# Forgetting attention on one core: the gates' rows on ScalarE's DMA queue, the weight piece asked for at unit 0

## The chip, the core and the metric

The kernel runs on one core of a Trainium2 chip. The metric is the device time of one execution in microseconds (us). The core has five instruction streams: TensorE (PE; PEld is its weight load), VectorE (DVE), ScalarE (ACT), GpSimd (POOL) and SyncE (SP). Each executes its own instructions in their order and waits for the others on semaphores. DMAs are issued by SP, POOL or ACT, as instructions of that stream. A DMA that has to wait holds up everything behind it in the same stream.

## What is computed

A two-layer decoder trunk over 512 positions of width 1024. Layer 0 has dilated window attention, layer 1 has forgetting attention, and each is followed by a gated convolutional feed-forward part. The change lies in forgetting attention: 16 heads of width 64, causal, with a bias made of the cumulative log of the forget gates, c.

```python
def fox_mixer(xn, w_q, w_o, k, v, c):
    q = (xn @ w_q).reshape(B, T, B_HEADS, HEAD_DIM)
    ...
    for i in range(T // BLK):                       # BLK = 128 queries
        s = jnp.einsum('bqhd,bkhd->bhqk', q[:, q0:q1], k[:, :q1]) * scale
        s = s + (c_t[:, :, q0:q1, None] - c_t[:, :, None, :q1])
        s = jnp.where(causal, s, NEG)
        p = jax.nn.softmax(s, axis=-1)
        outs.append(jnp.einsum('bhqk,bkhd->bqhd', p, v[:, :q1]))
    return jnp.concatenate(outs, axis=1).reshape(B, T, B_WIDTH) @ w_o
```

## The kernel before

All products are made from split operands: each float32 matrix is a high part and a low part, and a product is three matmuls (`mm3`, lines 267 to 269).

**The stage.** Forgetting attention runs over 32 units, (j,i) for head pair j = 0..7 and query block i = 0..3; unit (j,i) sees 128(i+1) keys. The loop over n (line 1585 on) is a software pipeline written out by hand, and each engine executes its instructions in the order in which the loop body issues them. For unit n the body issues: the scores on PE (`f_scores`, line 1509); the division of unit n-1 by its row sums on DVE (`f_norm`, 1528 and 1530); the biased scores and their maximum on DVE (1518) and the exponentials on ACT (1520), both in `f_exp`; the bias of unit n+1 on POOL (`f_bias`, 1492 and 1493); a quarter of the query projection of a later pair on PE (`q_part`); the transposes of unit n-2 on PE with their copies on ACT (`f_transpose`, 1542 and 1544). Every fourth unit the products with the values of the preceding pair are made (`f_pv`, 1557).

**The gates' rows (ck).** The cumulative gates lie in DRAM as 16 rows of 512 (`cd`). `load_ck(j)` (line 1399) reads the two rows of pair j into all 128 partitions, 512 KB, in one DMA on SP's queue (1402). Pair j+1's rows are asked for at unit (j,0). Their readers are the four biases of pair j+1; the first of these is issued at unit (j,3).

**The query copies (qst).** At unit (j,0) ACT makes the high part of the queries of pair j+1 (1426), at (j,1) DVE the low part (1434). Then two DMAs swap the halves between partitions 0-63 and 64-127 (1437, 1438). They are on SP's queue for pairs 1 to 6, on POOL's for 0 and 7. The scores of unit (j+1,0) need them.

**The weight pieces (wraw).** `Weights` brings every weight in pieces of 512 KB. `load(n)` issues DMAs on SP's queue (46) until n pieces are under way; `high` (54) first calls `load` for its own piece and `ahead_dma` (here 1) more, then rounds a piece to its high part on ACT. The low part is a subtraction on DVE (`low`, 66), or, in pairs 2 to 5, a negated copy on ACT (`minus`, 61) and an accumulating DMA from POOL's queue which reads the raw piece (`low_added`, 81). `high` runs at unit (j,1) of pairs 0 and 1, at the end of unit (j,0) of pairs 2 to 5, and at (6,1), (6,2) and (6,3) of the last pieces; `low_added` at unit (j,1).

**Buffers.** The tiles wraw, ck, bias and prob (the probabilities of a unit) share one pool, t4, of ten buffers. A new tile takes a buffer whose last reader is done; whichever instruction writes it first waits for that reader. A raw piece is freed by its low part, ck by the last bias of its pair (issued at (j,2)), a bias by its unit's step on DVE, prob by its transposes two units later.

Of the kernel before, what the change touches and what calls it, by code (L numbers as in the profile page):

```python
# [15 lines left out]
T = 512  # L16
# [84 lines left out]
def trunk_kernel(ctx, tc, x, norm_gains, w_qkv_a, w_o_a, w_q_b, w_o_b, kv_norm, w_kvf, b_f,  # L101
                 w_up, conv_w, conv_b, w_down, rope, out):
    nc = tc.nc
    act, dve, pool, pe, sp = nc.scalar, nc.vector, nc.gpsimd, nc.tensor, nc.sync
# [8 lines left out]
    def t8(shape, dt=F32, name="t8"):  # L113
        return p8.tile(shape, dt, tag="t8", name=name)

    def t4(shape, dt=F32, name="t4"):
        return p4.tile(shape, dt, tag="t4", name=name)
# [82 lines left out]
    W = Weights(nc, new_raw, lambda: t8([128, 2, 1024], F32R, name="w"), pieces)  # L200
# [1157 lines left out]
    def values(banks, w, s, blocks):  # L1358
        for b in blocks:
            for k in range(2):  # L1360
                kc = 2 * s + k
                ah, al = xs(bd2.xT, kc, slice(b * 128, b * 128 + 128))
                mm3(banks[b], ah, al, w[0][:, k, :], w[1][:, k, :], kc == 0, kc == KD - 1)

    def value_weight():
        return [t.rearrange("p (k c) -> p k c", k=2) for t in W.get()]
# [29 lines left out]

    cks = {}

    def load_ck(j):
        t = t4([128, 2, T], name="ck")  # L1400
        s = cd[2 * j:2 * j + 2, :]
        sp.dma_start(t, bass.AP(tensor=s.tensor, offset=s.offset, ap=[[0, 128], [T, 2], [1, T]]))
        cks[j] = t

    qT = {}
# [2 lines left out]
    def q_part(j, i):  # L1408

        if j >= 8:  # L1410
            return
        if i == 0:
            qps[j] = (bank([128, T], name="q_ps"), [t.rearrange("p (k c) -> p k c", k=8) for t in W.get()])
        o, (wh, wl) = qps[j]
        for kc in (2 * i, 2 * i + 1):
            bh, bl = xs(xTq, kc, ALL)
            mm3(o, wh[:, kc, :], wl[:, kc, :], bh, bl, kc == 0, kc == KD - 1)

    def q_high(j):
        if j >= 8:  # L1420
            return
        o = qps[j][0]
        qT[j] = t = t8([128, 2, 2, T], F32R, name="qst")
        for hh in range(2):
            own, _ = halves(hh)
            act.copy(t[own, 0, hh], o[own])

    def q_low(j):
        if j >= 8:
            return  # L1430
        o, t = qps.pop(j)[0], qT[j]
        for hh in range(2):
            own, other = halves(hh)
            dve.tensor_tensor(t[other, 0, hh], o[own], t[own, 0, hh].bitcast(F32), ALU.subtract)

        queue = sp if 0 < j < 7 else pool
        queue.dma_start(t[0:64, 1].bitcast(F32), t[64:128, 0].bitcast(F32))
        queue.dma_start(t[64:128, 1].bitcast(F32), t[0:64, 0].bitcast(F32))
# [26 lines left out]
    for s in range(4):  # L1465
        values(banks, value_weight(), s, range(4))
        next(down1, None)
        if s == 0:
            W.ahead = 2
            q_part(0, 0)  # L1470
            q_part(0, 1)
            load_ck(0)
        elif s == 1:
            q_part(0, 2)
        elif s == 2:
            q_part(0, 3)
            q_high(0)
            q_low(0)
# [8 lines left out]
    def f_bias(j, i):  # L1487
        n = (i + 1) * 128
        bias = t4([128, 2, T], name="bias")
        for hh in range(2):  # L1490
            hd = 2 * j + hh
            pool.tensor_scalar(bias[:, hh, :n], cks[j][:, hh, :n], -1.0, cq[:, i, hd:hd + 1], ALU.mult, ALU.add)
        pool.affine_select(bias[:, :, n - 128:n], bias[:, :, n - 128:n], pattern=[[0, 2], [-1, 128]],
                           compare_op=ALU.is_ge, fill=NEG, base=0, channel_multiplier=1)
        bia[j, i] = bias

    def f_scores(j, i):
        n = (i + 1) * 128
        nn = max(n, 256)
        if i < 2:  # L1500
            o = bank([128, 2, 256], name="s_ps")
            s = [o[:, hh] for hh in range(2)]
        else:
            s = [bank([128, T], name="s_ps") for _ in range(2)]
        for hh in range(2):
            hd = 2 * j + hh
            k = kst[hd // 4][:, hd % 4, :nn]
            for m in range(2):
                pe.matmul(s[hh][:, :nn], qT[j][:, m, hh, i * 128:(i + 1) * 128], k, start=m == 0, stop=m == 1)  # L1509
        return s  # L1510

    def f_exp(j, i, s):
        n = (i + 1) * 128
        bias = bia.pop((j, i))
        p = t4([128, 2, T], name="prob")
        nm, ls = small(2, "nm"), small(2, "ls")
        for hh in range(2):
            dve.tensor_tensor_reduce(p[:, hh, :n], s[hh][:, :n], bias[:, hh, :n], -0.125, BIG, ALU.add, ALU.min,
                                     nm[:, hh:hh + 1])
            act.activation(p[:, hh, :n], p[:, hh, :n], AF.Exp, bias=nm[:, hh:hh + 1], scale=-1.0,  # L1520
                           accum_out=ls[:, hh:hh + 1])
        prob[j, i] = (p, ls)

    def f_norm(j, i):
        n = (i + 1) * 128
        p, ls = prob[j, i]
        rl = small(2, "rl")
        dve.reciprocal(rl, ls)
        for hh in range(2):
            dve.tensor_scalar(p[:, hh, :n], p[:, hh, :n], rl[:, hh:hh + 1], None, ALU.mult)  # L1530
# [3 lines left out]
    def f_transpose(j, i):  # L1534
        p, _ = prob.pop((j, i))
        for hh in range(2):
            if i >= 2 or hh == 0:
                o = bank([128, 4, 128], name="pT_ps")
                t = t2([128, 4, 128], name="pT")
            k0 = (i + 1) * hh if i < 2 else 0  # L1540
            for k in range(i + 1):
                pe.transpose(o[:, k0 + k, :], p[:, hh, k * 128:(k + 1) * 128], ident)  # L1542
            if i >= 2 or hh == 1:
                act.copy(t[:, :k0 + i + 1], o[:, :k0 + i + 1])
            pT[j, i, hh] = t[:, k0:k0 + i + 1]
# [4 lines left out]
    def f_pv(j, i):  # L1550
        if i == 0:
            ops[j] = bank([128, T], name="o_ps")
        o = ops[j]
        for k in range(i + 1):
            for hh in range(2):
                hd = 2 * j + hh
                pe.matmul(o[64 * hh:64 * hh + 64, i * 128:(i + 1) * 128],  # L1557
                          Vt[hd // 8][:, k, (hd % 8) * 64:(hd % 8) * 64 + 64], pT[j, i, hh][:, k, :],
                          start=k == 0, stop=k == i)
        del pT[j, i, 0], pT[j, i, 1]  # L1560

    def f_out_high(j):
        o = ops[j]
        if j % 2 == 0:
            OTb[j // 2] = t8([128, 2, 2, T], F32R, name=f"OTb{j // 2}")
        t = OTb[j // 2]
        act.copy(t[:, 0, j % 2, :], o)

    def f_out_low(j):
        o, t = ops.pop(j), OTb[j // 2]  # L1570
        dve.tensor_tensor(t[:, 1, j % 2, :], o, t[:, 0, j % 2, :].bitcast(F32), ALU.subtract)
# [13 lines left out]
    for n in range(N + 3):  # L1585
        live = n < N
        if live:
            j, i = units[n]
            if i == 0 and j + 1 < 8:
                load_ck(j + 1)  # L1590
            s = f_scores(j, i)
        if 1 <= n <= N:
            f_norm(*units[n - 1])
        if live:
            f_exp(j, i, s)
            if n + 1 < N:
                f_bias(*units[n + 1])
            if i == 1:
                q_low(j + 1)
                if 2 <= j < 6:  # L1600
                    W.minus()
                    W.low_added()
            if i == 2 and j < 2 or (j, i) >= (6, 2):
                W.low()
            if i == 3 and j:
                f_out_low(j - 1)
            q_part(j + 1 + (i > 0), (i + 3) % 4)
        if 2 <= n < N + 2:
            f_transpose(*units[n - 2])
        if n >= N + 3 - len(fill):  # L1610
            po.both(*fill[n - N - 3 + len(fill)])

        if n % 4 == 2 or n == N:
            while pv_next < n - 2:
                ju, iu = units[pv_next]
                pv_next += 1
                f_pv(ju, iu)
                if iu == 3:
                    f_out_high(ju)
        if live and i == 0:  # L1620
            q_high(j + 1)
        if live and (i == (j < 2) if j < 6 else (j, i) >= (6, 1) and W.n_split < wo + 4):
            W.high()
# [51 lines left out]
```

## Time and profile before

| | |
|---|---|
| time, three runs | 1121.34, 1122.23, 1122.56 us; median 1122.23 |
| the profiled execution's own time | 1121.25 us |
| its span in the profile | 1119.2 us |
| granted TensorE clock, mean | 0.998 |
| the edited stage | about 627 to 735 us of the span |
| ScalarE busy over the whole span | 615.7 us, 55% |

Times in the profile are counted from the start of the span. A row of a timeline gives start, duration, engine, line, operation, tile written and tiles read, the number of instructions merged into the row, and in brackets the idle time of the engine just before it with what ended that time. "SPq" is the instruction stream of SP: the duration of such a row is that of the issue, not of the transfer. A row of waits gives who waited for whom, the sum in us, how often, and the longest. Busy times of PE are modelled ends of pipelined matmuls.

### The profile page before, as it was taken

To read this page: it belongs to the slowest core of one execution; us is meant where nothing else is said; L and a number is where in the kernel's file an instruction comes from. 1 tells how busy PE (TensorE), PEld (TensorE's weight loads), DVE (VectorE), ACT (ScalarE), POOL (GpSimd) and SP (SyncE) were. 2 spreads that over 40 slices of the span, in tenths; PEclk is the share of its full clock that TensorE was granted. 3 is DMA by queue.
4 is the path that set the end of the run, shared out by engine and by line. 5 is a ranking of instruction groups with operands and counts; after the bars stand their busy time and mean duration, and the time that the engine had idled before them with its cause. 6 is when DMAs were issued, how large, how long until landed. Compare 5 with 4: busy or idle time off the path is not lost. (4 is left out here: it accounts for less than half of the span.)

```text
span 1119.2 us, 17259 instructions
## 1 busy us (share of the span) xinstructions
PE 1108.2 (99%) x6259; PEld 950.2 (85%) x6259; DVE 891.1 (80%) x1453; ACT 615.7 (55%) x1036; POOL 182.7 (16%) x277
## 2 busy tenths in 40 slices
PE   9999999999999999999999999999999999999997
PEld 6988889889899888888878888789889889888886
DVE  6577788888888689997697777848888888589994
ACT  5444575545445457576462688745445445456572
POOL 1832101200000121000001545500300000121000
PEclk9999999999999999999999999999999999999999
DMA  9469864343433699893447666374333443599862
GB/s 323 149 212 407 323 176 134 94 119 104 139 121 116 158 359 368 299 323 110 132 151 273 198 165 169 105 207 130 96 102 115 132 125 121 151 352 368 319 245 75
DMA packets 179183, 217.34 MB, mean 194 GB/s; under 512 B 11225, under 2 KB 131017, under 8 KB 179098
## 3 DMA queue, kind: packets, MB, share of 16 engines
q1 hardware_dynamic: 169594, 183.99, 50.2%
q0 software_dynamic: 9504, 32.25, 9.1%
q8 instruction: 49, 0.80, 0.3%
q14 instruction: 36, 0.29, 0.1%
HBM read 166.08 MB, written 39.63 MB: 184 GB/s over the span
## 5 line engine op out<-in xcount | busy, mean ns | idle before, releaser
L597 ACT ACTIVATE bb<-up,conv 128x512 f32<-128x512 f32 x80 | 60.6, 775 | 148.6 <-DVE up L927 76.2
L66 DVE TENSOR_TENSOR w<-wraw,w 128x1024 fp32r<-128x1024 f32 x98 | 125.1, 1306 | 18.3 <-ACT w L54 17.8
L267 PE MATMUL acc<-w 128*128 128x512 f32 (+1 forms) x311 | 120.7, 388 | 0.3 <-DVE mix L314 0.3
L269 PE MATMUL acc<-w 128*128 128x512 f32 (+1 forms) x311 | 120.5, 388 | 0.1
L54 ACT CAST w<-wraw 128x1024 fp32r<-128x1024 f32 x110 | 111.5, 1047 | 15.8 <-PE v_ps L268 6.9
L267 PE MATMUL up<-xbh,w 128*128 128x512 f32 (+1 forms) x292 | 104.9, 359 | 0.0
L268 PE MATMUL up<-xcl,w 128*128 128x512 f32 (+1 forms) x292 | 104.9, 359 | 0.0
L267 PE MATMUL up<-xch,w 128*128 128x512 f32 (+1 forms) x292 | 104.9, 359 | 0.0
L268 PE MATMUL up<-xbl,w 128*128 128x512 f32 (+1 forms) x292 | 104.9, 359 | 0.0
L269 PE MATMUL up<-xbh,w 128*128 128x512 f32 (+1 forms) x292 | 104.7, 359 | 0.0
L269 PE MATMUL up<-xch,w 128*128 128x512 f32 (+1 forms) x292 | 104.7, 359 | 0.0
L268 PE MATMUL acc<-w 128*128 128x512 f32 (+1 forms) x267 | 103.3, 387 | 0.0
L613 POOL DMA_DIRECT2D hD<-hc x42 | 24.2, 577 | 317.7 <-DVE hc L615 316.6
L267 PEld LDWEIGHTS acc<-w 128*128 128x128 f32 x311 | 58.4, 188 | 12.6 <-DVE mix L314 0.7
L269 PEld LDWEIGHTS acc<-w 128*128 128x128 f32 x311 | 58.4, 188 | 12.4 <-DVE w L725 0.6
L598 DVE SCALAR_TENSOR_TENSOR bb<-up,conv,bb 128x511 f32<-128x511 f32 x80 | 59.5, 744 | 7.7 <-ACT bb L597 7.7
L268 PE MATMUL up<-xsl,w 128*128 128x256 f32 x224 | 63.4, 283 | 0.0
L267 PE MATMUL up<-xsh,w 128*128 128x256 f32 x224 | 63.4, 283 | 0.0
L269 PE MATMUL up<-xsh,w 128*128 128x256 f32 x224 | 63.4, 283 | 0.0
L267 PEld LDWEIGHTS up<-xbh,w 128*128 128x128 f32 x292 | 55.1, 189 | 8.3
L600 DVE SCALAR_TENSOR_TENSOR bb<-up,conv,bb 128x510 f32<-128x510 f32 x80 | 59.9, 749 | 2.8
L267 PEld LDWEIGHTS up<-xch,w 128*128 128x128 f32 x292 | 55.1, 189 | 8.3
(303 smaller groups left out, 3017.5 us busy)
## 6 DMA issues: line engine op xcount, KB each, us to landing
wraw<-in_w_up_dram SPq DMA_DIRECT2D x88, 512.0 KB
dT<-dsums SPq DMA_DIRECT2D x24, 512.0 KB
dsums<-in_w_down_dram SPq DMA_DIRECT2D x22, 512.0 KB
dsums<-in_w_down_dram SPq DMA_DIRECT2D x44, 256.0 KB
hD<-hc POOLq DMA_DIRECT2D x44, 256.0 KB, 4.7
dact<-hD SPq DMA_DIRECT2D x44, 256.0 KB
wraw<-dT SPq DMA_DIRECT2D x22, 512.0 KB
wraw<-in_w_down_dram SPq DMA_DIRECT2D x22, 512.0 KB
```

Of the source, the lines that this page charges most:

```text
L54: self.nc.scalar.copy(pair[:, 0], raw)
L66: self.nc.vector.tensor_tensor(pair[:, 1], raw, pair[:, 0].bitcast(F32), ALU.subtract)
L267: pe.matmul(o, ah, bh, start=first, stop=False, skip_group_check=shared)
L268: pe.matmul(o, ah, bl, start=False, stop=False, skip_group_check=shared)
L269: pe.matmul(o, al, bh, start=False, stop=last, skip_group_check=shared)
L597: act.activation(bb[:, s, :], ps, AF.Identity, bias=cp[:, 3, ch:ch + 1], scale=cp[:, 2, ch:ch + 1])
L598: dve.scalar_tensor_tensor(bb[:, s, 1:], ps[:, :T - 1], cp[:, 1, ch:ch + 1], bb[:, s, 1:], ALU.mult, ALU.add)
L600: dve.scalar_tensor_tensor(bb[:, s, 2:], ps[:, :T - 2], cp[:, 0, ch:ch + 1], bb[:, s, 2:], ALU.mult, ALU.add)
L613: pool.dma_start(hD[c - 1], hc.pop(c - 1))
```

## The change

`load_ck` takes the queue as an argument. The load of pair 0, ahead of the loop, stays on SP's queue; the seven loads in the loop are issued by ACT. At the same place, unit 0 of pairs 0 to 6, `W.load` is called for as many pieces as the next `high` would ask for, so that `high` finds its DMA already issued.

```diff
-    def load_ck(j):
+    def load_ck(j, queue):
         t = t4([128, 2, T], name="ck")
         s = cd[2 * j:2 * j + 2, :]
-        sp.dma_start(t, bass.AP(tensor=s.tensor, offset=s.offset, ap=[[0, 128], [T, 2], [1, T]]))
+        queue.dma_start(t, bass.AP(tensor=s.tensor, offset=s.offset, ap=[[0, 128], [T, 2], [1, T]]))
         cks[j] = t
...
             q_part(0, 1)
-            load_ck(0)
+            load_ck(0, sp)
...
             j, i = units[n]
             if i == 0 and j + 1 < 8:
-                load_ck(j + 1)
+                load_ck(j + 1, act)
+                W.load(W.n_split + 1 + W.ahead_dma)
             s = f_scores(j, i)
```

## The prediction

> **What bounds the kernel now.** I read the page first, then the waits of TensorE over the whole span, then the chain of waits and the timelines of the forgetting-attention stage (627 to 735 us), because only that stage is edited.
>
> ```profile
> span 1119.2 us, 17259 instructions
> PE 1108.2 (99%) x6259; PEld 950.2 (85%) x6259; DVE 891.1 (80%) x1453; ACT 615.7 (55%) x1036; POOL 182.7 (16%) x277
> ```
>
> TensorE (PE) is busy for all but 11 us of the span. No edit that removes waits can gain more than that, and only waits inside this stage are in reach. These are the ones of the stage:
>
> ```profile
> PE s_ps L1509 <- DMA qst<-qst: 1.3, 3, 0.7
> PE pT_ps L1542 <- ACT w L54: 0.6, 1, 0.6
> ```
>
> Three times the scores wait for the copies of the query pair between partitions (qst), once a transpose waits. The timeline of PE places them; I call unit i of head pair j "(j,i)".
>
> ```profile
> 635.87 0.36 PE L1509 MATMUL s_ps<-kst,qst 128*128 128x256 f32 x1
> 636.45 0.59 PE L1509 MATMUL s_ps<-kst,qst 128*128 128x256 f32 x3 [0.21 <-DMA qst<-qst]
> ...
> 649.17 0.36 PE L1509 MATMUL s_ps<-kst,qst 128*128 128x256 f32 x1
> 649.86 0.59 PE L1509 MATMUL s_ps<-kst,qst 128*128 128x256 f32 x3 [0.33 <-DMA qst<-qst]
> ...
> 662.58 0.71 PE L1509 MATMUL s_ps<-kst,qst 128*128 128x256 f32 x4
> ...
> 675.42 0.72 PE L1509 MATMUL s_ps<-kst,qst 128*128 128x256 f32 x4
> ...
> 711.71 0.28 PE L1509 MATMUL s_ps<-kst,qst 128*128 128x256 f32 x1
> 712.70 0.60 PE L1509 MATMUL s_ps<-kst,qst 128*128 128x256 f32 x3 [0.71 <-DMA qst<-qst]
> ...
> 716.47 1.30 PE L1542 MATMUL pT_ps<-ident,prob 128*128 128x128 f32 x8 [0.62 <-ACT w L54]
> ```
>
> Matmuls overlap, so the bracket understates a stall. Undisturbed, four scores take 0.71 us and the last alone 0.28, so they follow each other at (0.71 - 0.28)/3 = 0.14 us. The real stalls are 636.45 - 635.87 - 0.14 = 0.44 us at (1,0), 649.86 - 649.17 - 0.14 = 0.55 at (2,0), and 0.85 at (7,0). Without stalls PE needs 675.42 - 662.58 = 12.84 us for a head pair. ScalarE (ACT) and VectorE (DVE) pass each unit's softmax to and fro at the same pace: the first exponential of pairs 3 and 4 is 677.19 - 664.38 = 12.81 us apart.
>
> ```profile
> 662.91 0.59 ACT L1544 COPY pT<-pT_ps 128x512 f32<-128x512 f32 x1
> 664.38 0.40 ACT L1520 ACTIVATE prob<-prob,nm 128x128 f32<-128x128 f32 x1 [0.89 <-DVE nm L1518]
> ...
> 677.19 0.40 ACT L1520 ACTIVATE prob<-prob,nm 128x128 f32<-128x128 f32 x1 [0.85 <-DMA ck<-cd]
> ```
>
> So two chains of nearly equal length run side by side, and late in the stage it is the softmax chain that holds PE, as the chain of waits shows:
>
> ```profile
> 703.86 1.14 POOL bias L1492 x2
> 705.79 0.68 DVE qst L1434
> ...
> 707.80 1.82 issue
> 709.61 0.56 DVE prob L1518
> ...
> 716.47 0.63 PE pT_ps L1542 x4
> ```
>
> From 703.86 to 716.47 the path runs over GpSimd (POOL), DVE and ACT. At 716.47 PE has caught up with the softmax of (6,3), whose scaling on DVE is this row:
>
> ```profile
> 715.84 1.22 DVE L1530 TENSOR_SCALAR prob<-prob,rl 128x512 f32<-128x512 f32 x2
> ```
>
> The first of its two halves ends near 716.45, and PE goes on at 716.47; I put the wait down to that, not to the cast that the bracket names. After it PE has no stall to the end of the stage. This point is where I weigh everything: what PE wins before it is lost again there, and what the softmax chain loses before it comes out at the end.
>
> **The change, part by part.** Seven loads of the gates' rows (ck, pairs 1 to 7) leave SyncE (SP) and go to ACT; ck of pair 0 stays. For SP that is seven issues less. In pairs 0 and 1 the next weight piece (wraw) is asked for at unit 0 instead of 1, in pairs 2 to 5 at the start instead of the end of unit 0, in pair 6 at unit 0 instead of 1. Bytes and arithmetic stay.
>
> *The query copies.* On SP the order around them is now:
>
> ```profile
> 631.75 0.53 SPq L1437 DMA_DIRECT2D qst<-qst  x1
> 632.44 0.48 SPq L1438 DMA_DIRECT2D qst<-qst  x1
> 632.97 0.60 SPq L46 DMA_DIRECT2D wraw<-in_w_q_b_dram  x1
> 633.66 1.31 SPq L1402 DMA_DIRECT2D ck<-cd  x1
> ...
> 658.43 0.33 SPq L1402 DMA_DIRECT2D ck<-cd  x1
> 662.09 0.38 SPq L46 DMA_DIRECT2D wraw<-in_w_q_b_dram  x1
> 668.74 0.47 SPq L1437 DMA_DIRECT2D qst<-qst  x1
> ```
>
> The pair of 256 KB copies issued at 631.75 is followed within 2 us by a 512 KB piece and 512 KB of ck, and lands only for 636.45. After the change ck starts some 6 us later and the stalls of 0.44 and 0.55 us should go: 0.99 us for PE. From below the gain is 0, if the copies are slow by themselves; I take 0.99 for PE, but 0 for the end, because PE then only waits longer for the softmax chain up to 716.47. The 0.85 at (7,0) belongs to copies issued by POOL, which are not edited. [...]
>
> *The issue on ACT.* No DMA is issued from ACT in this trace; the nearest row is that of the same load on SP (minimum, median, maximum in ns):
>
> ```profile
> L1402 SPq DMA_DIRECT2D ck<-cd x8: 332/358/2105, 596.6 to 696.8; - x8
> ```
>
> From below the issue costs 0, from above 2.10 us. I take the 0.33 us of the ck at 658.43, the issue that follows no other within 2 us. Its place on ACT is between the copy that ends at 662.91 + 0.59 = 663.50 and the exponential at 664.38, where ACT waits 0.89 us for DVE. So 0.33 us costs nothing; without that cover it is 7 x 0.33 = 2.3 us. Behind it in ACT's order are the two exponentials of (j,0), for which DVE waits.
>
> *The buffers.* Tile t4 has ten buffers for wraw, ck, bias and prob. The rows show who takes whose:
>
> ```profile
> 657.69 0.90 POOL L81 DMA_DIRECT2D w<-wraw  x1 [3.39 <-ACT w L61]
> ...
> 660.08 0.52 POOL L1493 TENSOR_SCALAR_AFFINE_SELECT bias<-bias 128x256 f32<-128x256 f32 x1
> ...
> 665.73 0.98 POOL L1492 TENSOR_SCALAR bias<-ck,cq 128x256 f32<-128x256 f32 x2 [3.85 <-DMA w<-wraw]
> ...
> 670.39 0.89 POOL L81 DMA_DIRECT2D w<-wraw  x1 [1.59 <-ACT w L61]
> ...
> 673.29 0.81 POOL L1492 TENSOR_SCALAR bias<-ck,cq 128x128 f32<-128x128 f32 x2
> ```
>
> The bias of (3,1) at 665.73 waits until the accumulating copy issued at 657.69 has read its raw piece: it got that piece's buffer. In the order of asking (ck, prob, bias, wraw) the buffers come from bias (2,2), ck of pair 2, the raw piece, bias (2,3). With wraw moved ahead of prob and bias, the weight takes ck's old buffer (free at about 660.6 instead of the 662.09 of its issue now; the copies behind it on SP come only at 668.74), prob of (3,0) takes the raw piece's, bias (3,1) that of (2,3). So the wait on the accumulating copy moves from POOL to DVE, to the first softmax step of each pair from 3 to 6:
>
> ```profile
> 664.01 0.28 DVE L1518 CUSTOM_DVE_ANT_0 prob<-s_ps,bias 128x128 f32<-128x128 f32 x1
> 676.82 0.28 DVE L1518 CUSTOM_DVE_ANT_0 prob<-s_ps,bias 128x128 f32<-128x128 f32 x1
> DMA to landing us min/median/max: 6.2/6.4/7.9
> ```
>
> (The last row is the tile view of wraw, for its four accumulating copies.) DVE needs the buffer 664.01 - 657.69 = 6.32 us after the issue in pair 3 and 676.82 - 670.39 = 6.43 in pair 4. The median landing of 6.4 just fits; the slowest, at 665.73, does not, by 665.73 - 664.01 = 1.72 us. Behind DVE's wait are that unit's exponentials on ACT and the whole chain. The price is between 0, if the first copy lands at 6.3 too now that no ck starts 0.74 us behind it, and 1.72, if it stays as it is. Nothing in the trace tells the two apart, since the weight piece now starts 2.9 us behind it instead of 4.4; I take the middle, 0.9 us, and 0 for pairs 4 to 6, which lie at the median. POOL's freedom is worth nothing, as its bias is not what ACT waits for. The gates' rows come in time: those of pair 4, asked for at 663.5 instead of 658.43, are first read by POOL at 673.29, 9.8 us later, and no landing above is longer than 7.9.
>
> *Sum.* Query copies 0, issue 0, buffers +0.9: span 1120.1, and with the 1121.25 - 1119.2 = 2.05 us around it 1122.15. The profiled execution lies 0.98 under the median of 1122.23, so the forecast for a median is 1122.23 + 0.9 = 1123.1 us. A measurement of this kernel can tell about 0.2%, 2.2 us, from no change.
>
> **The rivals.**
>
> *PE keeps its gain.* If the softmax chain follows PE rather than itself, the 0.99 us come out in full: 1121.2. With the stalls at (7,0) and 716.47 (0.85 + 0.62) gone as well it would be 1119.8. For it speaks that the chain of waits runs over PE alone from 649.86 to 703; against it, that ACT waits for DVE and never for PE before its exponentials.
>
> *Each accumulating copy lands late.* The weight piece now runs beside it 1.5 us earlier. If all four land at the 7.9 us of the slowest, DVE waits 1.72 + 3 x (7.9 - 6.43) = 6.1 us, 1128.3. It decides from landings above 6.4. For it: the one that is already there. Against: the ck that ran beside these copies is gone, the same 512 KB.
>
> *ACT is held at its issue.* Where issues on SP stand close together they take longer (ck: 1.31 us at 633.66, 0.33 at 658.43). If ACT's issues are held like that beside SP's, each takes up to 2.10 us, 1.21 more than the 0.89 of cover: 7 x 1.21 = 8.5, 1130.7 us; it decides from 0.89. Against: SP issues nothing between 662.09 and 668.74, and ACT's turn is at 663.5. [...]
>
> *The change doesn't do what it says.* In pair 1 the weight piece is still issued straight behind the query copies, as it is asked for at (1,0), after SP's copies of (0,1). If the piece and not ck delays them, the stalls stay: 1122.2.
>
> **How the numbers follow.** Forecast (a loss of 0 to 1.9 us) 0.54; PE keeps its gain 0.20; late landings 0.12; ACT held 0.05; nothing happens 0.09. Slower by over 0.2% are late landings, ACT held and a rest of the forecast: 0.19. Faster by over 0.2% needs at least two of the stalls after 703 gone as well: 0.05. The rest, 0.76, is within. The range goes from 1121.0, just under the kept gain, to 1126.0, which leaves out most of the late landings; the forecast's own is 1122.2 to 1124.1.
>
> **What would show it.** Right: ck issues on ACT of 0.3 to 0.5 us before the exponentials of (j,0) with no later start of them; the brackets at (1,0) and (2,0) gone; POOL's waits for w<-wraw gone and DVE waiting at (3,0); a longer PE wait near 716. Wrong: stalls on PE's projections (pv) behind late copies of ACT, an issue on ACT above 0.9 us, or POOL still waiting for w<-wraw, which would mean that the buffers are handed out otherwise.

## The result, and the profile after

Over 22 runs each the changed kernel takes 1123.28 us (median) and the kernel before 1121.34: a ratio of 1.0017, 95% interval 1.0011 to 1.0022, so 1.9 us slower. The forecast was 1123.1. Of that agreement 0.9 us is luck: the three runs shown ahead of the prediction had a median of 1122.23, the 22 have 1121.34, so the predicted loss was 0.9 us and the measured one is 1.9.

The profiled execution after took 1123.22 us. Its page begins:

```profile
span 1121.3 us, 17231 instructions
PE 1109.4 (99%) x6259; PEld 950.1 (85%) x6259; DVE 890.3 (79%) x1453; ACT 614.4 (55%) x1036; POOL 182.6 (16%) x277
```

The work is the same; PE is busy 1.2 us longer by the record and the span is 2.1 us longer. The stage itself can be measured from the first scores of (0,0) to the start of the last products with the values. Before, from the timeline of PE, with the second of two issues on POOL that matter below:

```profile
620.76 0.51 POOL L1438 DMA_DIRECT2D qst<-qst  x1 [0.20 <-issue]
...
627.18 0.64 PE L1509 MATMUL s_ps<-kst,qst 128*128 128x256 f32 x4
...
733.32 1.75 PE L1557 MATMUL o_ps<-pT,Vt 128*64 128x128 f32 x28
```

After, the same rows and those that answer to the prediction's:

```profile
613.70 7.23 SPq L46 DMA_DIRECT2D wraw<-in_w_q_b_dram  x2
...
621.37 0.51 POOL L1438 DMA_DIRECT2D qst<-qst  x1 [0.20 <-issue]
...
627.78 0.28 PE L1509 MATMUL s_ps<-kst,qst 128*128 128x256 f32 x1
629.64 0.59 PE L1509 MATMUL s_ps<-kst,qst 128*128 128x256 f32 x3 [1.58 <-DMA qst<-qst]
...
638.29 0.92 PE L1509 MATMUL s_ps<-kst,qst 128*128 128x256 f32 x4
...
651.50 0.75 PE L1509 MATMUL s_ps<-kst,qst 128*128 128x256 f32 x4
...
661.01 1.58 PE L1557 MATMUL o_ps<-pT,Vt 128*64 128x128 f32 x16 [0.20 <-ACT pT L1544]
...
714.83 0.80 PE L1509 MATMUL s_ps<-kst,qst 128*128 128x256 f32 x4
...
719.38 1.30 PE L1542 MATMUL pT_ps<-ident,prob 128*128 128x128 f32 x8 [0.62 <-ACT w L54]
...
736.23 1.75 PE L1557 MATMUL o_ps<-pT,Vt 128*64 128x128 f32 x28
```

The stage takes 733.32 - 627.18 = 106.14 us before and 736.23 - 627.78 = 108.45 after: 2.31 us more. The remaining difference of the two spans lies outside (the stage starts 0.60 later, and what follows it is 0.81 shorter); the profiled runs differ by as much among each other there.

The stalls at (1,0), (2,0) and (7,0) are gone or nearly so: the four scores stand in one row of 0.92, 0.75 and 0.80 us. The 0.71 us of an undisturbed row leave 0.2 us of the 0.44 at (1,0) and less at the other two. A new stall stands at (0,0): 629.64 - 627.78 - 0.14 = 1.72 us. The scores there wait for the query copies of pair 0, which POOL issues, the second at 621.37. Beside them SP now issues the weight piece asked for at (0,0): the merged row at 613.70 holds two pieces, and its end, 620.93, is that of the second. The tile view of qst, cut to these copies, gives the time from issue to landing, first before and then after:

```profile
DMA to landing us min/median/max: 6.2/6.3/6.3
```

```profile
DMA to landing us min/median/max: 6.9/7.5/8.1
```

Before, the second copy landed 6.3 us or less behind 620.76. Its reader is the second of the four scores that begin at 627.18, so it stood at 627.18 + 0.14 = 627.32, 6.56 behind. There was a margin of 0.3 us at most and no stall to show it. After, the copy lands at 621.37 + 8.1 = 629.47, and PE goes on at 629.64.

The softmax chain carries this to the end. The timeline of ACT after:

```profile
630.70 0.41 ACT L1520 ACTIVATE prob<-prob,nm 128x128 f32<-128x128 f32 x1 [3.96 <-DVE nm L1518]
...
665.13 0.71 ACT L1520 ACTIVATE prob<-prob,nm 128x512 f32<-128x512 f32 x1
665.64 0.33 ACTq L1402 DMA_DIRECT2D ck<-cd  x1
...
665.84 0.56 ACT L1544 COPY pT<-pT_ps 128x512 f32<-128x512 f32 x1
667.47 0.40 ACT L1520 ACTIVATE prob<-prob,nm 128x128 f32<-128x128 f32 x1 [1.07 <-DVE nm L1518]
...
720.26 0.40 ACT L1520 ACTIVATE prob<-prob,nm 128x128 f32<-128x128 f32 x1 [1.00 <-DVE nm L1518]
```

and before, the two of these rows that the prediction did not show:

```profile
628.28 0.40 ACT L1520 ACTIVATE prob<-prob,nm 128x128 f32<-128x128 f32 x1 [2.15 <-DVE nm L1518]
...
717.35 0.40 ACT L1520 ACTIVATE prob<-prob,nm 128x128 f32<-128x128 f32 x1 [1.00 <-DVE nm L1518]
```

Without the 0.60 of the later start, the first exponential is 630.70 - 628.28 - 0.60 = 1.82 us late, that of (3,0) 667.47 - 664.38 - 0.60 = 2.49, that of (7,0) 720.26 - 717.35 - 0.60 = 2.31. So 1.8 us are lost at (0,0), some 0.7 in pairs 0 to 2, and nothing after. The chain of waits shows the same from the other side: from 653 to 719 it now runs over ACT, DVE, POOL and two loads of weight pieces, where before it ran over PE from 649.86 to 703.

```profile
653.58 1.06 issue
654.64 0.88 ACT prob L1520 x4
...
718.32 0.96 ACT w L54
719.38 0.63 PE pT_ps L1542 x4
```

The issue on ACT at 665.64 begins while the exponential of 665.13 still runs, and the copy behind it starts at 665.84 as that one ends. It takes no slot of ACT's own. The chain of waits passes through this issue on its way to DVE's reciprocal at 665.96, but it costs nothing there: DVE goes on 0.83 us behind the start of that exponential, as it does before (663.01 behind 662.18). By the view of line 1402 all seven issues are as short:

```profile
L1402 ACTq DMA_DIRECT2D ck<-cd x7: 326/326/344, 624.0 to 704.2; - x7
```

### The profile page after: what moved, and what is told of

Same layout as the page of the kernel before. It is cut to its first block, busy times and chain, and to the rows that moved or that the text cites. A ratio compares the mean times of both kernels' runs of the same rounds, so it can differ in the third digit from the quotient of the medians.

```text
span 1121.3 us, 17231 instructions
## 1 busy us (share of the span) xinstructions
PE 1109.4 (99%) x6259; PEld 950.1 (85%) x6259; DVE 890.3 (79%) x1453; ACT 614.4 (55%) x1036; POOL 182.6 (16%) x277
```

## The experiments

Each was timed in five rounds beside the kernel before. "Stage" is measured as above in the profiled run. "Copies 0" is the landing of the query copies of pair 0, least and longest, from the tile view of qst; it is empty for e5 and e13, where SP issues them and the profile has no landing for them. A profiled run can lie at the edge of its kernel's times: those of e7, e12 and e13 are the longest of each, those of e3 and e11 the shortest.

| run | edit, against the changed kernel unless it says before | median us | ratio, 95% interval | stage us | copies 0 us |
|---|---|---|---|---|---|
| before | | 1121.34 | 1 | 106.14 | 6.2 to 6.3 |
| after | the change | 1123.28 | 1.0017, 1.0011 to 1.0022 | 108.45 | 6.9 to 8.1 |
| e1 | queue alone | 1122.08 | 1.0010, 1.0001 to 1.0018 | 106.48 | 3.5 to 3.6 |
| e2 | weight piece alone | 1124.03 | 1.0025, 1.0015 to 1.0034 | 108.30 | 5.6 to 7.5 |
| e3 | no piece at (0,0) | 1121.71 | 1.0002, 0.9993 to 1.0011 | 106.68 | 3.0 to 3.4 |
| e4 | rows of pair 1 on SP | 1122.88 | 1.0017, 1.0008 to 1.0026 | 107.82 | 6.7 to 7.6 |
| e5 | copies 0 on SP | 1123.86 | 1.0022, 1.0013 to 1.0031 | 109.08 | |
| e13 | e5, piece behind the bias | 1123.73 | 1.0022, 1.0012 to 1.0031 | 109.53 | |
| e7 | before, piece at unit 0 from pair 1 | 1121.90 | 1.0006, 0.9997 to 1.0015 | 107.99 | 6.2 to 6.3 |
| e9 | e3, piece behind the bias | 1121.37 | 1.0000, 0.9991 to 1.0009 | 106.51 | 3.8 |
| e6 | e3, copies 7 on SP | 1119.80 | 0.9985, 0.9976 to 0.9994 | 105.33 | 3.4 to 3.6 |
| e10 | e9, copies 7 on SP | 1120.47 | 0.9991, 0.9982 to 1.0000 | 105.32 | 3.5 to 3.9 |
| e11 | before, copies 7 on SP | 1121.12 | 0.9999, 0.9990 to 1.0008 | 106.25 | 5.6 to 5.7 |
| e12 | e11, piece at (6,0) | 1118.80 | 0.9975, 0.9965 to 0.9986 | 104.65 | 5.6 to 5.7 |

### Which part makes the loss

**e1**, the queue alone:

```diff
                 load_ck(j + 1, act)
-                W.load(W.n_split + 1 + W.ahead_dma)
```

> Only the queue of the gates' rows is changed; the weight piece is asked for where it was. Theory A (the loss of about 2 us is made at (0,0): the weight piece asked for there is issued by SP at 620.6 us, beside the pair-0 query copies that POOL issues at 620.64, and makes them land late): no stall of 1.72 us in the scores of (0,0), first exponential within 0.3 us of 628.3 plus the run's own offset, ratio 0.999 to 1.000. Theory B (the gates' rows of pair 1, now issued by ACT at 623.98, hold up those copies): stall of 1 to 2 us stays, ratio 1.0015 to 1.0020. Theory C (the prediction's: buffers shifted by the earlier weight piece): the buffers fall as before, POOL again waits for the accumulating copies, no loss, ratio 1.000. Theory D (each issue on ACT lies on its path): 7 x 0.33 = 2.3 us, ratio 1.002.

**e2**, the weight piece alone (the loads of the rows stay on SP):

```diff
-                load_ck(j + 1, act)
+                load_ck(j + 1)
                 W.load(W.n_split + 1 + W.ahead_dma)
```

> Only the weight piece is asked for at unit 0; the gates' rows stay on SP, just ahead of it. Theory A: the scores of (0,0) wait 1.2 to 2 us as in the changed kernel, the first exponential is late by as much, ratio 1.0010 to 1.0020; the stalls at (1,0) and (2,0) may stay, as SP again issues the rows at the same unit. Theory B: no stall at (0,0), ratio 0.999 to 1.000. Theory C: POOL's waits for the accumulating copies gone, DVE late at (3,0) by up to 0.9 us, ratio up to 1.0008. Theory D: no issue on ACT, ratio 1.000.

**e3**, no piece at (0,0):

```diff
-                W.load(W.n_split + 1 + W.ahead_dma)
+                if j:
+                    W.load(W.n_split + 1 + W.ahead_dma)
```

> The whole change, but for pair 0: there the weight piece is asked for at unit 1, as before. Theory A: the stall at (0,0) is gone and with it the loss, ratio 0.999 to 1.000; what PE gains at (1,0) and (2,0), 0.99 us, is waited for again where the transposes of (6,3) meet the softmax, so not below 0.999. Theory B: stall stays, 1.0015 to 1.0020. Theory C: as the changed kernel, 1.0008 to 1.0020. Theory D: 1.002.

**e4**, the rows of pair 1 on SP:

```diff
-                load_ck(j + 1, act)
+                load_ck(j + 1, act if j else sp)
```

> The whole change, but the gates' rows of pair 1 are issued by SP, as before. Theory A: the stall of 1.2 to 2 us at (0,0) stays, ratio 1.0010 to 1.0020. Theory B: the stall is gone, ratio 0.999 to 1.000. Theory C: as the changed kernel, up to 1.0017. Theory D: six issues of 0.33 us on ACT, ratio 1.0017.

The loss follows the piece at (0,0): it is there in e2 and e4, gone in e3, and smaller in e1. The scores of (0,0) stall in e2 by 1.10 us, in e4 by 1.15, and not at all in e1 and e3. Theory A holds. B falls as the main cause with e4, where the rows of pair 1 are back on SP and the stall stays. It is 1.15 us there and not 1.72, so rows issued by ACT while the copies are in flight (623.98 after) may add to it; no run singles out their share. C and D fall with e3, where the buffers of pairs 3 to 6 go round as in the changed kernel and all seven issues stand on ACT. In the column of landings the copies of pair 0 take 3.0 to 3.9 us with neither the rows of pair 1 from SP nor the piece beside them, 5.6 to 6.3 with the rows, up to 8.1 with the piece. In e1 the interval lies above 1, which A did not expect; its stage is only 0.34 us longer, the copies of pair 7 stalling PE by 1.91 us instead of 0.85 and the wait of 0.62 at 716 being gone. The timeline of PE in e1 also says what delayed the copies of pairs 1 and 2:

```profile
635.97 0.36 PE L1509 MATMUL s_ps<-kst,qst 128*128 128x256 f32 x1
636.49 0.60 PE L1509 MATMUL s_ps<-kst,qst 128*128 128x256 f32 x3 [0.15 <-DMA qst<-qst]
...
649.21 0.36 PE L1509 MATMUL s_ps<-kst,qst 128*128 128x256 f32 x1
649.95 0.59 PE L1509 MATMUL s_ps<-kst,qst 128*128 128x256 f32 x3 [0.38 <-DMA qst<-qst]
```

The gates' rows are away from SP here and the piece still follows the copies: stalls of 0.38 and 0.60 us, as before. In e2 the rows follow at once and the piece 1.4 us later or more, and the four scores stand in one row of 0.97 and 0.90 us, so 0.2 to 0.3 us of each stall is left. PE also reaches these scores a little sooner or later behind the copies from run to run (5.84 us behind the first issue at (2,0) before, 5.30 in e2), so the stalls compare the landings only roughly.

### Is it the copies' own queue?

**e5**, the copies of pair 0 issued by SP:

```diff
-        queue = sp if 0 < j < 7 else pool
+        queue = sp if j < 7 else pool
```

> The whole change, but the query copies of pair 0 are issued by SP, just ahead of the weight piece of (0,0), and not by POOL beside it. If the copies only lose to the bytes that move beside them, whichever stream issues: they still land late, a stall of 0.4 to 1.5 us at (0,0), ratio 1.0004 to 1.0015. If it is the copies issued by POOL that lose against a transfer issued by SP: landing back to 6.3 us or less, no stall, ratio 0.9990 to 1.0005. Prediction's buffers: unchanged, 1.0017.

Neither case came as written. The stall at (0,0) is gone, but the time is no better. The profile has no landing for these two copies; the four scores stand in one row from 626.66, so the second copy, issued at 619.98, had landed 6.8 us behind at the latest, where it took up to 8.1 after. How fast these copies are on SP is therefore open. The timelines of e5, DVE and PE:

```profile
631.74 0.42 DVE L1518 CUSTOM_DVE_ANT_0 prob<-s_ps,bias 128x256 f32<-128x256 f32 x1 [2.00 <-DMA dT<-dsums]
...
635.36 0.36 PE L1509 MATMUL s_ps<-kst,qst 128*128 128x256 f32 x1
637.64 0.59 PE L1509 MATMUL s_ps<-kst,qst 128*128 128x256 f32 x3 [1.92 <-DMA qst<-qst]
```

The piece asked for at (0,0) takes a buffer of t4, and so prob of (0,1) gets the next one: that of dsums, a tile of the feed-forward part which comes from t4 too and which POOL's store to dT (issued at 624.28) still reads. DVE waits 2.00 us for the store; the low part of the next queries comes behind it, so the copies of pair 1 are late and PE stalls 637.64 - 635.36 - 0.14 = 2.14 us at (1,0). In e6, e1 and e3, which ask for no piece at (0,0), it is POOL's bias of (0,2) that waits for this store, 0.28, 0.36 and 1.00 us. So the piece at (0,0) does harm in two ways which lie over each other: after, where the first scores come 1.72 us late, DVE doesn't wait for the store. With one mended, the other shows.

**e13** was to take away this second harm by asking for the piece behind the bias:

```diff
-                W.load(W.n_split + 1 + W.ahead_dma)
             s = f_scores(j, i)
...
                 f_bias(*units[n + 1])
+            if i == 0 and j < 7:
+                W.load(W.n_split + 1 + W.ahead_dma)
```

> As the run with the first query copies on SP, but the piece is asked for behind the bias in all pairs, pair 0 too. There the softmax of (0,1) on DVE waited 2.0 us for the store of dT from dsums, whose buffer its prob had been given because the weight piece had taken the one before. If the order of asking does that: prob gets the buffer it had before, DVE's wait of 2.0 us goes, the stall of 2.1 us at (1,0) behind it falls under 0.2, ratio 0.9990 to 1.0003; the piece itself waits on SP for the store. If the store would be late for DVE in any order, or the wait belongs to the piece's bytes: ratio 1.0015 to 1.0025 again.

DVE waits 2.17 us for the store again. The expectation had the order wrong: prob of (0,1) is asked for at the next unit, behind the piece in either place. The wait follows the order of buffers, but the run doesn't tell its two cases apart. One more buffer in t4 might; it wasn't tried.

### What the queue change and the earlier piece are worth

**e7**, the rows back on SP, the piece at unit 0 from pair 1 on:

```diff
-                load_ck(j + 1, act)
-                W.load(W.n_split + 1 + W.ahead_dma)
+                load_ck(j + 1)
+                if j:
+                    W.load(W.n_split + 1 + W.ahead_dma)
```

> The gates' rows stay on SP, the weight piece is asked for at unit 0 from pair 1 on only: the kernel that left out pair 0, without the queue change. Tells what the queue itself is worth. If the queue matters through the accumulating copies (the rows issued beside them): these land in 6.2 us or more again and DVE waits for the buffer of prob at (3,0) and (4,0), 0.2 to 0.5 us in sum, as where only the piece was moved; ratio 1.0003 to 1.0010. If the queue is worth nothing: 1.0002, no late step at (3,0). Stalls of PE at (1,0) and (2,0) gone in both cases if the weight piece, not the rows, delayed those copies; there again (0.4 to 0.55) if it was the rows.

The profiled run of e7 shows the wait that the prediction counted on at (3,0). The timeline of DVE and the landing of the accumulating copies (tile view of wraw) in e7:

```profile
665.68 0.29 DVE L1518 CUSTOM_DVE_ANT_0 prob<-s_ps,bias 128x128 f32<-128x128 f32 x1 [1.13 <-PE pT_ps L1542]
...
678.80 0.29 DVE L1518 CUSTOM_DVE_ANT_0 prob<-s_ps,bias 128x128 f32<-128x128 f32 x1 [0.19 <-DMA w<-wraw]
```

```profile
DMA to landing us min/median/max: 6.2/6.4/7.4
```

The bracket of the first row names PE, but the copy issued at 658.02 lands 7.4 us later, at 665.4, and DVE starts at 665.68. In the changed kernel, where ACT issues the rows 5.0 us behind that copy (665.64 against 660.64) and not 0.7, the four copies land faster, and no wait is left:

```profile
DMA to landing us min/median/max: 4.7/4.8/5.1
```

The row of DVE at (3,0) after has no bracket:

```profile
667.10 0.28 DVE L1518 CUSTOM_DVE_ANT_0 prob<-s_ps,bias 128x128 f32<-128x128 f32 x1
```

So these landings are shorter with the rows on ACT: their median is 4.6 to 4.8 us in after, e1, e3, e5, e6 and e9, and 6.2 to 6.4 in before, e2, e7, e11 and e12, where they are on SP. No run tells the distance from the queue. What the shorter landings are worth in time is not settled: the stages of the two profiled runs, e7 and e3, differ by 1.31 us, but that of e7 is its longest run, and the medians differ by 0.2, within the intervals. The stalls at (1,0) and (2,0) stay in e7, 0.52 and 0.55 us: at (1,0) the piece follows the copies, at (2,0) the rows do, 0.6 us behind the second copy, and the piece behind them.

**e9** put the piece of pairs 1 to 6 behind the bias:

```diff
-                W.load(W.n_split + 1 + W.ahead_dma)
             s = f_scores(j, i)
...
                 f_bias(*units[n + 1])
+            if i == 0 and 0 < j < 7:
+                W.load(W.n_split + 1 + W.ahead_dma)
```

> The rows on ACT's queue and the piece at unit 0 from pair 1 on, but asked for behind the bias and not ahead of the scores, so that the buffers go round as before the change. If POOL's bias, freed from its waits, runs beside DVE's scaling of prob and stretches it (0.88 to 1.03 us for 512 wide, 0.75 to 0.98 for 384 in pair 0, between the queue-only kernel and the one with the piece from pair 1 on): the waits of POOL for transposes and accumulating copies come back, the scaling of (0,3) is 0.88 us again, the first three pairs of the softmax take 36.1 to 36.4 us instead of 36.8, and the ratio is 0.9993 to 1.0000. If the stretch has nothing to do with the order of buffers: 36.8 us and 1.0002.

POOL's waits for the accumulating copies came back (0.41 to 1.00 us), the ratio is 1.0000, but the scaling of (0,3) stays at 1.03 us, and the first three pairs take 664.80 - 628.26 = 36.54 us, between the two cases. They take 36.1 to 36.2 us in before, e11 and e12, 36.4 in e1, 36.8 in e3, e6, e10 and after. So the softmax chain is 0.4 to 0.7 us slower there in the kernels with the early piece. The rows say in part why. The timelines of POOL and DVE in e3, and then the same scaling, of (0,1), in before:

```profile
632.17 1.48 POOL L1492 TENSOR_SCALAR bias<-ck,cq 128x512 f32<-128x512 f32 x2
632.74 1.06 DVE L1530 TENSOR_SCALAR prob<-prob,rl 128x256 f32<-128x256 f32 x2
```

```profile
632.64 0.61 DVE L1530 TENSOR_SCALAR prob<-prob,rl 128x256 f32<-128x256 f32 x2
```

In before POOL has ended that bias and its mask at 632.53. From 626 to 680 us, in the profiles of before, after, e1, e3, e5, e6, e7, e11 and e12, a scaling of 128x256 takes 0.61 or 0.62 us where no POOL instruction runs beside it, and 0.66 to 1.06 where a bias or its mask does. The twelve scalings of the first three pairs take 9.12 us together in before, 9.53 in e3 and 9.60 after, most of the difference of 0.7 us. In e9 POOL's bias still runs beside the scaling of (0,3), so that edit did not take the cause away. What the rest is stays open.

### A better kernel

In the traces of before, after, e1, e3, e5 and e7, the scaling on DVE at (6,1) takes 2.15 or 2.16 us. **e6** tests whether POOL's issue of the copies of pair 7, at the same time, is the cause:

```diff
-        queue = sp if 0 < j < 7 else pool
+        queue = sp if 0 < j else pool
...
-                W.load(W.n_split + 1 + W.ahead_dma)
+                if j:
+                    W.load(W.n_split + 1 + W.ahead_dma)
```

> The piece at unit 0 from pair 1 on, and the query copies of pair 7 issued by SP instead of POOL. In every trace so far the scaling on DVE at (6,1) takes 2.16 us where it takes 0.62 in other pairs, while POOL issues those two copies (707.80 and 708.52 in the kernel with the piece from pair 1 on). If POOL's issuing stretches it, the scaling falls to 0.62 to 0.9 us, the softmax chain wins 1.2 to 1.5 us behind it, the copies land earlier (stall of 0.88 us at (7,0) gone or under 0.3), and since the softmax chain holds PE at the transposes of (6,3), the end is 0.6 to 1.5 us earlier: 1120.2 to 1121.1, ratio 0.9988 to 0.9997. If PE sets the end: only the stall at (7,0), up to 0.88, ratio 0.9994. If the stretch has another cause: 1.0002 as without the edit.

The timeline of DVE and POOL in e3, without this edit, and then the row of DVE in e6:

```profile
707.80 0.57 POOL L1437 DMA_DIRECT2D qst<-qst  x1 [1.80 <-DVE qst L1434]
708.45 2.16 DVE L1530 TENSOR_SCALAR prob<-prob,rl 128x256 f32<-128x256 f32 x2
708.52 0.53 POOL L1438 DMA_DIRECT2D qst<-qst  x1 [0.16 <-DVE rl L1528]
709.10 1.36 POOL L1492 TENSOR_SCALAR bias<-ck,cq 128x512 f32<-128x512 f32 x2
```

```profile
708.23 0.85 DVE L1530 TENSOR_SCALAR prob<-prob,rl 128x256 f32<-128x256 f32 x2
```

It is, by itself or by what it holds back. The scaling gets 1.31 us shorter, the stage 1.35, and the median is 1.9 us below that of e3. In e3 POOL's bias follows the issues from 709.10 to 710.46, and the scaling ends at 710.61; in e6 POOL doesn't wait for the low part of the copies, and that bias runs from 705.90 on, ahead of the scaling. So the run doesn't tell the issues from the bias behind them: the scaling takes 2.16 us while POOL issues and computes, and 0.85 when SP issues. How they stretch it is not shown.

**e10** joins e6 and e9, **e11** makes the same edit of the copies on the kernel before and no other:

```diff
-        queue = sp if 0 < j < 7 else pool
+        queue = sp if 0 < j else pool
```

> Both edits that helped: rows on ACT's queue, the piece at unit 0 behind the bias from pair 1 on, the query copies of pair 7 on SP. If the two gains add (0.34 us of median between the piece ahead of the scores and behind the bias, 1.9 us for the copies of pair 7): about 1119.4 us, ratio 0.9980 to 0.9985. If the copies of pair 7 are all there is: 1119.8, 0.9985. If POOL's waits for accumulating copies come back to the path: 0.9990 or above.

> The kernel before, with the query copies of pair 7 on SP and nothing else: tells whether that gain needs any part of the change. Scaling at (6,1) 0.6 to 0.9 us instead of 2.16; the stall of 0.85 us at (7,0) and the 0.62 at 716 gone. If the two stalls behind 703 are what PE can win: 0.85 + 0.62 = 1.5 us, ratio 0.9985 to 0.9990. If PE's earlier stalls at (1,0) and (2,0) set the end once the late ones are gone, and the earlier piece is therefore worth something again: 0.9990 to 0.9995, clearly above the kernel with the piece from pair 1 on (0.9985).

In e10 the gains don't add: the stage is as long as in e6 (105.32 against 105.33), and the intervals overlap. In e11 nearly nothing is won, though the scaling takes 0.69 us there. The timelines of SP and ACT in e11 show who took it:

```profile
706.91 0.46 SPq L1438 DMA_DIRECT2D qst<-qst  x1
707.47 2.65 SPq L46 DMA_DIRECT2D wraw<-in_w_o_b_dram  x3
...
712.97 1.05 ACT L54 CAST w<-wraw 128x1024 fp32r<-128x1024 f32 x1 [2.49 <-DMA wraw<-in_w_o_b_dram]
```

SP waits for the low part and issues the copies from 706.22 us on. Behind them stand the last three weight pieces, ACT waits 2.49 us for one of them, and behind ACT the softmax of (6,3). In e6 the first of the three had been asked for at (6,0), ahead of the copies. **e12** adds that alone to e11:

```diff
                 load_ck(j + 1)
+                if j == 6:
+                    W.load(W.n_split + 1 + W.ahead_dma)
```

> The kernel before with the query copies of pair 7 on SP, and the weight piece asked for at unit 0 in pair 6 only; the rows stay on SP. In the run with the copies alone, SP waits for the copies' low part until 706.2 us and issues the last weight pieces only from 707.47 on, so that ScalarE waits 2.49 us for one at 712.97 and gives back what the copies won. If that is all, ScalarE's wait goes here, the transposes of (6,3) start within 0.5 us of 716.1 and the ratio is 0.9983 to 0.9990, as with the whole of the other edits. If the rows on ACT's queue or the earlier pieces of pairs 1 to 5 are needed as well: 0.9993 or above.

ACT's wait is gone, and the transposes of (6,3) wait 0.30 us. The timeline of PE in e12:

```profile
712.75 0.64 PE L1509 MATMUL s_ps<-kst,qst 128*128 128x256 f32 x4
...
716.20 1.10 PE L1542 MATMUL pT_ps<-ident,prob 128*128 128x128 f32 x8 [0.30 <-DVE prob L1530]
```

With 1118.80 us, ratio 0.9975 (0.9965 to 0.9986), it is faster than both kernels. Of the change it keeps one seventh, the piece at (6,0); the rows stay on SP and the pieces of pairs 0 to 5 where they were. Against e6 its stage is 0.68 us shorter, most of it in pairs 0 to 2; the intervals of the two ratios overlap.

## Why the prediction was right in its number, and where it was not

**Two chains; what PE wins is lost, what the softmax loses comes out.** Right, and shown from both sides. In e3 the stalls at (1,0) and (2,0), 0.99 us, are gone but for 0.1, and the stage is not shorter. The 1.82 us that the softmax chain loses at (0,0) stand undiminished at (7,0). But 716 is not the only point where PE is caught. It waits for pT at 661.01 after, and at 659.09 in e3:

```profile
649.53 0.72 PE L1509 MATMUL s_ps<-kst,qst 128*128 128x256 f32 x4
...
659.09 1.14 PE L1557 MATMUL o_ps<-pT,Vt 128*64 128x128 f32 x10 [0.30 <-ACT pT L1544]
...
663.36 0.72 PE L1509 MATMUL s_ps<-kst,qst 128*128 128x256 f32 x4
```

From (2,0) to (3,0) PE takes 663.36 - 649.53 = 13.83 us where it needs 12.84: the gain is given back within one pair, part of it at no bracket.

**The query copies.** The stalls of pairs 1 and 2 went, as said, but for 0.2 us. The reason given, that the rows start later, is only part of it: with only the piece behind the copies the stalls stayed (e1), with the rows close behind and the piece later most of them went (e2). In e7 0.55 us stayed at (2,0) with the rows first and the piece 1.5 us behind them, so the rows have a share. The 0.85 us at (7,0), which the prediction left where it was, went too: those copies land in 4.0 to 4.5 us after, 4.1 to 5.1 before. They take 5.3 in e3, with a stall of 0.88 us, and up to 6.3 in e1, with 1.91; no run singles out what delays them.

**The issue on ACT.** Right: 0.33 us, and nothing of it comes out on the path. The cover is better than the one named, since the issue begins beside the exponential ahead of it.

**The buffers: the step that failed.** "So the wait on the accumulating copy moves from POOL to DVE", at 0.9 us for (3,0), taken as the middle of 0 and 1.72. The wait left POOL, and on DVE it is 0, the lower bound: the copies land in 4.8 us instead of 6.4. The bound's own reason, that no rows start beside the copy any more, fits e7 (a median of 6.4 us, 7.4 for the first copy and 1.13 us of wait with the rows back). It is not all of it for the first copy, the one that the 1.72 came from: in e1, with the rows away too, that one took 6.1 us and the others 4.5 to 4.7. "POOL's freedom is worth nothing" fails as well: freed from its waits, POOL works beside DVE's scalings, which take 0.5 us longer over the first three pairs.

**What the sum left out.** The part on query copies looked at those on SP, and passed over pair 0's, on POOL, as not edited. The piece at (0,0) was named as moved, but not followed to what runs beside it at 620 us, nor to the buffer that prob of (0,1) then gets. By the rows of before, the margin there was 6.56 - 6.3 = 0.3 us at most. This term is 1.7 to 1.8 us where the sum had 0, and the term in its place was 0.9 where the runs show 0. The forecast loss was so 0.9 us where 1.9 were measured, and only because the three runs stood 0.9 high did 1123.1 come out beside 1123.28: the number is luck, and the mechanism that made it was another.

**The rivals.** PE did not keep its gain. The accumulating copies landed earlier, not later. ACT was not held: its longest issue is 344 ns. The change did what it says. Of the signs named, two did not come: DVE doesn't wait at (3,0), and the wait of PE near 716 is no longer than before (0.62 us at 719.38, as at 716.47), since PE waits earlier, at 629.64 and 661.01. The sign that decided, a stall at (0,0), was not among them.

## What to carry to other kernels

A transfer that is asked for earlier has to be followed to three places: what else is in flight at its new time and with what margin that lands (a reader that just doesn't wait is the one to look at: a margin of 0.3 us became a stall of 1.72 here), which buffer it takes and who gets the next one (DVE's wait of 2.00 us in e5), and what stands behind it on its queue. Of the two chains that run at one pace here, stalls of 0.99 us taken from one were worth nothing (e3), while a delay of 1.82 put on the other came out whole; so look first for what stretches the slower one, here scalings on DVE beside what POOL issues and computes (2.16 us against 0.85 at (6,1)). A DMA moved to another queue can give back there what it won, as the weight pieces behind the copies on SP did: ACT waited 2.49 us for one in e11.

## What had not been expected of the hardware

Two 256 KB copies between partitions, issued by POOL, landed for pair 0 in 3.0 to 3.9 us, in 5.6 to 6.3 or in up to 8.1, by what SP had issued before or beside them; accumulating copies of 512 KB in a median of 4.8 us after and 6.4 in e7. A DMA issue on ACT took 0.33 us and overlapped the exponential ahead of it. Two DMA issues on POOL, with the bias behind them, went with a scaling on DVE of 2.16 us instead of 0.85, and a bias of POOL beside a scaling with 1.06 us instead of 0.61.
